# Layer 1's value rows in seven buffers, four of them borrowed from the rings of split up-projection weights

## The chip, the cores and the metric

The kernel runs on one core of one Trainium2 chip. The metric is the device time of the whole program in microseconds. The time before is the median of three runs, 2615.96 us (2612.59 to 2622.68).

## The reference

The program is a model of two layers over 256 tokens and 256 context tokens of width 1024. Each layer has a mixer (a convolution, a neighbourhood attention and a grouped attention over shared projections) and a PEER feed-forward, which is the part that matters here. For each token it picks, for each of 8 heads, 16 of 16384 experts by product keys, and then computes

```
act = gelu(einsum('cd,chkd->chk', xc, take(u, idx)))
out = einsum('chk,chkd->cd', g * act, take(v, idx))
```

so `u` and `v` are 16384 x 1024 tables of float32, `idx` are the picked experts and `g` the softmax of their scores. In the last layer only the 256 tokens go on, and the context does not.

## The kernel before

**How the work is tiled.** Most tokens are computed densely: the 16384 experts are cut into 128 blocks of 128, and each block is computed for all of these tokens, with a gate that is zero for experts that weren't picked. In layer 1 there are 192 dense token columns (`nd`): 128 of one tile and 64 of the other. The other 64 tokens take the rows of u and v that they picked by indirect DMA (names `gru` and `grv`), 64 steps each, and VectorE multiplies and sums them (L914, L921).

**A block of the sweep.** For block e, `act` multiplies the block's u (`raw_u`, 512 KB, plain float32) by the tokens in eight matmuls at L630, and ScalarE takes the gelu at L633 into `gact`. VectorE multiplies by the gates (L827; the gates come from DRAM as `gr`, eight blocks at a time, L825). ScalarE and VectorE split the product into two fp32r parts, `whi` (L831) and `wlo` (L832). The block's v (`raw_v`, 512 KB) is split in the same way into `hi_v` (L97) and `lo_v` (L99). For the first 128 tokens six fp32r matmuls (L119 to L121, into `acc`) multiply the parts; for the other 64 two plain ones at L842 use `raw_v` and `gact` themselves. In the texts U, R and A stand for the matmuls of L630, L842 and L119 to L121 of a block.

**Ahead of the sweep.** Layer 1 computes U of blocks 0 to 39 early, while VectorE still sorts and routes: eight stay in SBUF, 32 are spilled to DRAM (`gsp`, `spilled`) and come back as `gback` (L719). U of blocks 40 to 127 runs inside the sweep.

**Buffers.** All loads go through rings of `ring`, two or three buffers by tag:

```
raw = ring.tile(shape, F32, tag="raw" + kind, name="raw_" + nm, bufs=3)
hi = ring.tile(shape, F32R, tag="hi" + kind, name="hi_" + nm)
lo = ring.tile(shape, F32R, tag="lo" + kind, name="lo_" + nm)
```

Kind "v" has `rawv` (three buffers), `hiv` and `lov` (two each); kind "u" has `rawu`, `hiu` and `lou`. Each buffer holds 4 KB per partition. In layer 1 u isn't split, so nothing uses `hiu` and `lou` after the last split of the query weights (`piece(a["w_q"]...)`, L656). `rawv` is also used by the routing, for one-hot tiles (L792), up to the sweep's start.

**What sets the order.** Each engine, and SP's DMA queue, works through its instructions in one order, written when the program is built. The building tool places an instruction by its own estimate of when its operands and buffers will be free. A buffer's next load waits until the last reader of what it held is done, and all that stands behind it on SP waits with it. `hold` adds dependencies by hand: the gate product of block e waits for `wlo` of block e - 2, and a gather waits for the gate product of its block. The rings of `whi`, `wlo`, `hi_v` and `lo_v` have two buffers, so block e's need A of block e - 2 to be done.

Of the kernel before, what the change touches and what calls it, by code (L numbers as in the profile page):

```python
# [11 lines left out]
F32 = mybir.dt.float32  # L12
# [9 lines left out]
P = 128  # L22
T = 256
D = 1024
# [19 lines left out]
GA = {0: 4, 1: 8}  # L44
SPILL = {0: 42, 1: 32}
GLAG = 3
GB = 8
WOV = {0: (0, 1), 1: (1, 1)}
ZAT = (0, 2, 4, 6, 7, 9)
# [3 lines left out]
def hymba_kernel(ctx: ExitStack, tc: tile.TileContext, a, out):  # L53
    nc = tc.nc
# [4 lines left out]
    ring = ctx.enter_context(tc.tile_pool(name="ring", bufs=2))  # L59
# [26 lines left out]
    def hold(ins, after):  # L86

        if after is not None:
            tc.add_manual_dep(ins.ins, after.ins.name,
                              mybir.DependencyInfo(mybir.DependencyClass.Sync, mybir.DependencyReason.DATA),  # L90
                              reason="work that would crowd out more urgent work")


    def split(raw, shape, kind, nm, lo_eng=None, after=None):
        hi = ring.tile(shape, F32R, tag="hi" + kind, name="hi_" + nm)
        lo = ring.tile(shape, F32R, tag="lo" + kind, name="lo_" + nm)
        S.activation(hi, raw, AF.Copy)  # L97
        if lo_eng is None or lo_eng is V:
            V.tensor_tensor(lo, raw, hi.bitcast(F32), ALU.subtract)  # L99
        else:  # L100
            n = shape[1] // 4 if len(shape) == 3 and shape[1] == NC else 0
            for i in range(4):
                sl = (slice(None), slice(i * n, (i + 1) * n)) if n else (slice(None), i // 2, slice((i % 2) * 256, (i % 2 + 1) * 256))
                hold(lo_eng.tensor_tensor(lo[sl], raw[sl], hi[sl].bitcast(F32), ALU.subtract), after)  # L104
        return hi, lo

    def load(src, shape, kind, nm):
        raw = ring.tile(shape, F32, tag="raw" + kind, name="raw_" + nm, bufs=3)
        nc.sync.dma_start(raw, src)
        return raw  # L110
# [7 lines left out]
    def mm3(o, ahi, alo, bhi, blo, first, last):  # L118
        return [PE.matmul(o, lhsT=ahi, rhs=bhi, start=first, stop=False),  # L119
                PE.matmul(o, lhsT=ahi, rhs=blo, start=False, stop=False),  # L120
                PE.matmul(o, lhsT=alo, rhs=bhi, start=False, stop=last)]  # L121
# [17 lines left out]
    def squares(t, h):  # L139

        junk = cst.tile([P, 512], BF16, tag="sqj", name=f"sqj{t}{h}")
        S.activation(junk, resid[t][:, h * 512:(h + 1) * 512], AF.Square, accum_out=ssq[:, t, h:h + 1])
# [122 lines left out]
    def gate_rows(l, k, sets, tag="x2"):  # L265

        ns = mods[l][0].shape[-1] if len(sets) > 1 else 1
        ps = bank(tag, f"psrow{l}{k}")
        PE.transpose(ps[:NC * ns, :P], mod_of(l, k)[:, :, :ns].rearrange("p c s -> p (c s)"), ident)
        r = cst.tile([P, 256], F32, tag="sqj", name=f"gcol{l}{k}")  # L270
        S.activation(r[:NC * ns, :P], ps[:NC * ns, :P], AF.Copy)
        d = dram.tile([NC, ns, P], F32, name=f"growd{l}{k}")
        nc.sync.dma_start(d.rearrange("c s p -> (c s) p"), r[:NC * ns, :P])
        rows = {}
        for s in sets:
            rows[s] = cst.tile([P, D], F32, tag="grow", name=f"grow{l}{k}{s}", bufs=2)
            nc.sync.dma_start(rows[s].rearrange("p (c q) -> p c q", c=NC), d[:, s, :].partition_broadcast(P))
        return rows
# [311 lines left out]
    def peer(l):  # L590
# [120 lines left out]
        def act_of(e, sw, after):  # L711
# [5 lines left out]
            if i % 2 == 0:  # L717
                two[0] = sw.tile([P, 2, nd], F32, tag="gback", name=f"gback{l}_{e}", bufs=GB // 2)
                hold(nc.scalar.dma_start(two[0], spilled[:, i:i + 2, :]), after)  # L719
            return two[0][:, i % 2]  # L720

        sweep(l, dense, gath, act_of, h2n, eidx, gates, gd, nd, nb)

    def route(l, t, rt, rw, best, pos, tix, gate, gd, eidx, ntok):
# [84 lines left out]
    def sweep(l, dense, gath, act, h2n, eidx, gates, gd, nd, nb):  # L809
        sw = ctx_peer.enter_context(tc.tile_pool(name=f"sw{l}", bufs=2))  # L810
        pair = l == DEPTH - 1
# [9 lines left out]
        for e in range(NE):  # L821
            ga = act(e, sw, los[(e - GA[l]) // 2] if 0 <= e - GA[l] < GB else None)
            if e % EG == 0 and e >= NEAR[l]:
                gr = sw.tile([P, nb, EG, TB], F32, tag="gr", name=f"gr{l}_{e}")
                nc.scalar.dma_start(gr, gd[1][:, :, e:e + EG, :])  # L825
            g = gr[:, :, e % EG, :] if e >= NEAR[l] else gd[0][:, :, e, :]
            wi = V.tensor_tensor(ga[:, :nd].rearrange("p (b t) -> p b t", t=TB),  # L827
                            ga[:, :nd].rearrange("p (b t) -> p b t", t=TB), g, ALU.mult)
            whi = sw.tile([P, nw], F32R, tag="whi", name=f"whi{l}_{e}")
            wlo = sw.tile([P, nw], F32R, tag="wlo", name=f"wlo{l}_{e}")  # L830
            S.activation(whi, ga[:, :nw], AF.Copy)  # L831
            los.append(V.tensor_tensor(wlo, ga[:, :nw], whi.bitcast(F32), ALU.subtract))  # L832
            if e >= 2:
                hold(wi, los[e - 2])
            raw = load(a["v"][l, e], [P, D], "v", f"v{l}_{e}")
            v = split(raw, [P, D], "v", f"v{l}_{e}")

            def down_proj(j, h, e=e, whi=whi, wlo=wlo, v=v, ga=ga, raw=raw):
                ts, hs = slice(j * P, (j + 1) * P), slice(h * 512, (h + 1) * 512)
                if pair and j:  # L840

                    return [PE.matmul(acc[1][0][k * H:(k + 1) * H], lhsT=ga[:, P:P + H], rhs=raw[:, k * 512:(k + 1) * 512],  # L842
                                      start=e == 0, stop=e == NE - 1) for k in range(2)]
                return mm3(acc[j][h], whi[:, ts], wlo[:, ts], v[0][:, hs], v[1][:, hs], e == 0, e == NE - 1)

            if e < NE - 2:
                for j in range(len(dense)):
                    for h in range(len(acc[j])):
                        down_proj(j, h)
            else:  # L850
                last.append(down_proj)
            while steps and (e >= NE - 2 or ng - len(steps) < ng * (4 * e - 3 * min(e, ahead)) // (480 - 3 * ahead)):
                steps.pop(0)(wi)
            if e == NE - 12:
                rows = gate_rows(l, 5, [0, 1] if gath else [0], "mm")
            if e == NE - 2 and not pair:
                for g, t in enumerate(gath):
                    V.tensor_tensor(h2n[g], h2n[g], rows[t // 2], ALU.mult)
                    V.tensor_tensor(resid[t], resid[t], h2n[g], ALU.add)
                    for h in range(2):  # L860
                        squares(t, h)
# [22 lines left out]
        for j, t in [(1, 1), (0, 0)] if pair else enumerate(dense):  # L884
# [4 lines left out]
            if l == DEPTH - 1:  # L889
                y = sw.tile([P, D], F32, tag="grow", name=f"y{t}", bufs=GLAG + 1)  # L890
                y = [y[:, :512], y[:, 512:]]
# [7 lines left out]
    def gather_steps(l, gath, h2n, eidx, gates, sw, ns):  # L899
# [5 lines left out]
        def use(after):  # L905
            rows, f = waiting.pop(0)
            hold(f(rows), after)

        for g in range(len(gath)):
# [13 lines left out]
            def step(k, after, g=g, t=t, down=down, up=up):  # L923
                s = k % ns
                r = sw.tile([P, D], F32, tag="grow", name=f"gr{'uv'[k // ns]}{l}{t}{s}", bufs=GLAG + 1)
                d = G.indirect_dma_start(out=r, out_offset=None, in_=a["v_rows" if k >= ns else "u_rows"],  # L926
                                         in_offset=bass.IndirectOffsetOnAxis(ap=eidx[g][:, s:s + 1], axis=0))
                hold(d, after)
                waiting.append((r, lambda rows, s=s, f=up if k >= ns else down: f(s, rows)))
                if len(waiting) > GLAG:  # L930
                    use(after)
# [3 lines left out]
        if steps:  # L935
            steps.extend([use] * GLAG)
        return steps
# [89 lines left out]
```

## Time and profile before

| what | value |
|---|---|
| median of three runs | 2615.96 us |
| profiled execution, its own time | 2629.2 us |
| its span | 2627.1 us |
| PE busy | 95% of the span |
| DVE, ACT, POOL busy | 70%, 40%, 40% |
| HBM read, written | 628.63 MB, 49.44 MB |
| mean DMA rate | 259 GB/s |

Sums are made against the profiled execution, which is 13.2 us above the median. Engines: PE is TensorE's matmuls, PEld its weight loads, DVE VectorE, ACT ScalarE, POOL GpSimd, SP the queue that issues most loads. Layer 1's sweep runs from about 2005 us to 2615 us. An instruction's row gives its start, its length and, in brackets, how long its engine stood idle before it and what ended that. Neighbouring matmuls overlap, so the distance from start to start is what a matmul costs, not its length.

### The profile page before, as it was taken

To read this page: it belongs to the slowest core of one execution; us is meant where nothing else is said; L and a number is where in the kernel's file an instruction comes from. 1 tells how busy PE (TensorE), PEld (TensorE's weight loads), DVE (VectorE), ACT (ScalarE), POOL (GpSimd) and SP (SyncE) were. 2 spreads that over 40 slices of the span, in tenths; PEclk is the share of its full clock that TensorE was granted. 3 is DMA by queue.
4 is the path that set the end of the run, shared out by engine and by line. 5 is a ranking of instruction groups with operands and counts; after the bars stand their busy time and mean duration, and the time that the engine had idled before them with its cause. 6 is when DMAs were issued, how large, how long until landed. Compare 5 with 4: busy or idle time off the path is not lost. (4 is left out here: it accounts for less than half of the span.)

```text
span 2627.1 us, 38186 instructions
## 1 busy us (share of the span) xinstructions
PE 2491.1 (95%) x13837; PEld 2023.0 (77%) x13837; DVE 1831.6 (70%) x3506; ACT 1052.3 (40%) x1708; POOL 1050.9 (40%) x967
## 2 busy tenths in 40 slices
PE   7999999888899999999999998998998999999997
PEld 4755788877898888989989987855997756777775
DVE  1754589989546677787888885374994467666667
ACT  3345633367533333333333334445454333323323
POOL 3713434768642244454545441722600114223222
PEclk9999999999999999999999999998999999999999
DMA  7343364356878889999999992441579889999996
GB/s 270 104 169 122 127 245 145 119 211 263 311 257 276 293 295 328 326 343 339 347 331 342 338 336 85 161 164 49 159 241 344 278 286 326 377 356 361 350 366 234
DMA packets 263565, 681.42 MB, mean 259 GB/s; under 512 B 23840, under 2 KB 112976, under 8 KB 260304
## 3 DMA queue, kind: packets, MB, share of 16 engines
q1 hardware_dynamic: 121712, 423.48, 45.4%
q0 software_dynamic: 55296, 201.35, 20.8%
q10 hardware_dynamic: 86368, 54.15, 7.2%
q8 instruction: 109, 1.79, 0.3%
q14 instruction: 80, 0.66, 0.1%
HBM read 628.63 MB, written 49.44 MB: 258 GB/s over the span
## 5 line engine op out<-in xcount | busy, mean ns | idle before, releaser
L120 PE MATMUL acc<-lo_v,whi 128*128 128x512 f32 x1024 | 406.1, 397 | 2.9 <-DVE lo_v L99 2.8
L99 DVE TENSOR_TENSOR lo_v<-raw_v,hi_v 128x1024 fp32r<-128x1024 f32 x256 | 313.5, 1225 | 119.9 <-ACT hi_v L97 119.1
L630 PE MATMUL psu<-h2raw,raw_u 128*128 128x192 f32 x2048 | 364.9, 330 | 10.1 <-DMA raw_u<-in_u 6.3
L121 PE MATMUL acc<-hi_v,wlo 128*128 128x512 f32 x1024 | 374.4, 392 | 0.0
L97 ACT ACTIVATE hi_v<-raw_v 128x1024 fp32r<-128x1024 f32 x256 | 269.1, 1052 | 260.4 <-PE acc L121 234.5
L630 PEld LDWEIGHTS psu<-h2raw,raw_u 128*128 128x128 f32 x2048 | 339.8, 191 | 40.2 <-issue 20.7
L121 PE MATMUL psu<-ahi_m,lo_u 128*128 128x384 f32 x1024 | 351.7, 343 | 10.2 <-DVE lo_u L99 6.6
L119 PE MATMUL psu<-ahi_m,hi_u 128*128 128x384 f32 x1024 | 349.9, 342 | 7.0 <-ACT hi_u L97 2.9
L120 PE MATMUL psu<-alo_m,hi_u 128*128 128x384 f32 x1024 | 349.8, 342 | 0.0
L119 PE MATMUL acc<-hi_v,whi 128*128 128x512 f32 x1024 | 346.2, 404 | 2.9 <-ACT hi_v L97 2.7
L926 POOL DMA_INDIRECT gru<-in_u_rows,eidx x128 | 183.6, 1435 | 286.3 <-DVE gback L827 144.8
L119 PEld LDWEIGHTS acc<-hi_v,whi 128*128 128x128 f32 x1024 | 184.9, 188 | 104.1 <-ACT gact L633 55.2
L921 DVE SCALAR_TENSOR_TENSOR h2n<-grv,dots,h2n 128x1024 f32<-128x1024 f32 x190 | 243.0, 1279 | 26.0 <-DMA grv<-in_v,eidx 24.6
L914 DVE SCALAR_TENSOR_TENSOR gru<-gru,h2n 128x1024 f32<-128x1024 f32 x192 | 232.0, 1220 | 36.7 <-DMA gru<-in_u_rows,eidx 31.8
L104 POOL TENSOR_TENSOR lo_u<-raw_u,hi_u 128x256 fp32r<-128x256 f32 x184 | 213.1, 1190 | 95.2 <-ACT hi_u L97 84.0
L926 POOL DMA_INDIRECT grv<-in_v,eidx x128 | 171.3, 1338 | 188.3 <-DVE h2n L921 164.3
L926 POOL DMA_INDIRECT gru<-in_u_rows,egl x64 | 90.2, 1409 | 376.3 <-DMA spilled<-gsp 123.2
L120 PEld LDWEIGHTS acc<-lo_v,whi 128*128 128x128 f32 x1024 | 192.6, 188 | 55.8 <-issue 5.7
L121 PEld LDWEIGHTS acc<-hi_v,wlo 128*128 128x128 f32 x1024 | 192.3, 188 | 38.1 <-DVE wlo L832 0.3
L831 ACT ACTIVATE whi<-gact 128x128 fp32r<-128x128 f32 (+1 forms) x182 | 74.6, 410 | 337.2 <-PE acc L120 189.8
L121 PEld LDWEIGHTS psu<-ahi_m,lo_u 128*128 128x128 f32 x1024 | 195.7, 191 | 16.9 <-DVE lo_u L99 8.6
L119 PEld LDWEIGHTS psu<-ahi_m,hi_u 128*128 128x128 f32 x1024 | 195.8, 191 | 13.1 <-ACT gsp L633 3.5
(287 smaller groups left out, 4581.3 us busy)
## 6 DMA issues: line engine op xcount, KB each, us to landing
raw_u<-in_u SPq DMA_DIRECT2D x256, 512.0 KB, 5.6
raw_v<-in_v SPq DMA_DIRECT2D x256, 512.0 KB, 6.0
ada<-in_ada SPq DMA_DIRECT2D x96, 512.0 KB, 4.7
gd<-stage SPq DMA_DIRECT2D x24, 1024.0 KB, 5.5
gr<-gd ACTq DMA_DIRECT2D x16, 1536.0 KB, 25.2
raw_wq<-in_w_q SPq DMA_DIRECT2D x32, 512.0 KB, 3.6
raw_wout<-in_w_out SPq DMA_DIRECT2D x24, 512.0 KB, 3.5
gd<-stage SPq DMA_DIRECT2D x12, 960.0 KB, 5.8
```

The costliest lines, as they stand in the source:

```text
L97: S.activation(hi, raw, AF.Copy)
L99: V.tensor_tensor(lo, raw, hi.bitcast(F32), ALU.subtract)
L104: hold(lo_eng.tensor_tensor(lo[sl], raw[sl], hi[sl].bitcast(F32), ALU.subtract), after)
L119: return [PE.matmul(o, lhsT=ahi, rhs=bhi, start=first, stop=False), PE.matmul(o, lhsT=ahi, rhs=blo, start=False, stop=False), PE.matmul(o, ...
L120: PE.matmul(o, lhsT=ahi, rhs=blo, start=False, stop=False),
L121: PE.matmul(o, lhsT=alo, rhs=bhi, start=False, stop=last)]
L630: PE.matmul(ps[:, :nd], lhsT=u[:, c, :], rhs=h2raw[:, c, :nd], start=c == 0, stop=c == NC - 1)
L831: S.activation(whi, ga[:, :nw], AF.Copy)
L914: return V.scalar_tensor_tensor(r, r, 1.0, h2n[g], op0=ALU.mult, op1=ALU.mult, accum_out=dots[:, s:s + 1])
L921: return V.scalar_tensor_tensor(h2n[g], r, dots[:, s:s + 1], h2n[g], op0=ALU.mult, op1=ALU.add)
L926: d = G.indirect_dma_start(out=r, out_offset=None, in_=a["v_rows" if k >= ns else "u_rows"], in_offset=bass.IndirectOffsetOnAxis(ap=eidx[g ...
```

## The change

In layer 1 (`pair`) each v takes the next of seven buffers: two of `hiu`, two of `lou`, and the three of `rawv`. The tags repeat with period seven, so v of block e reuses the buffer of block e - 7. Nothing else is written differently; layer 0 loads as before. Line numbers are one higher in the changed kernel up to the new code in `sweep`, and seven higher behind it.

```diff
+VRING = (("hiu", 2), ("lou", 2), ("rawv", 3), ("hiu", 2), ("lou", 2), ("rawv", 3), ("rawv", 3))
...
-            raw = load(a["v"][l, e], [P, D], "v", f"v{l}_{e}")
+            if pair:
+
+                tag, bufs = VRING[e % len(VRING)]
+                raw = ring.tile([P, D], F32, tag=tag, name=f"raw_v{l}_{e}", bufs=bufs)
+                nc.sync.dma_start(raw, a["v"][l, e])
+            else:
+                raw = load(a["v"][l, e], [P, D], "v", f"v{l}_{e}")
             v = split(raw, [P, D], "v", f"v{l}_{e}")
```

The tool that builds the program writes another order for all engines but POOL from there on. On SP the first loads of u in layer 1 stand like this before (the number behind `raw_u_` is the block, the one behind it counts tiles):

```order
L109 DMA raw_wq_17662<-in_w_q 128x1024
L109 DMA raw_u_0_18440<-in_u 128x1024
L109 DMA raw_u_1_18453<-in_u 128x1024
L109 DMA raw_u_2_18466<-in_u 128x1024
L109 DMA raw_u_3_18479<-in_u 128x1024
L109 DMA raw_u_4_18492<-in_u 128x1024
```

and now:

```order
L110 DMA raw_wq_17662<-in_w_q 128x1024
L110 DMA raw_u_0_18440<-in_u 128x1024
L110 DMA raw_u_1_18453<-in_u 128x1024
L840 DMA raw_v_0_18974<-in_v 128x1024
L840 DMA raw_v_1_18993<-in_v 128x1024
L110 DMA raw_u_2_18466<-in_u 128x1024
L840 DMA raw_v_3_19031<-in_v 128x1024
L840 DMA raw_v_4_19052<-in_v 128x1024
L110 DMA raw_u_3_18479<-in_u 128x1024
L110 DMA raw_u_4_18492<-in_u 128x1024
```

Four loads of v, those that go into `hiu` and `lou`, moved from about sixty places further down to behind the last query weights.

PE in the middle of the sweep, around U of block 67, before:

```order
L630 MATMUL psu_66_20756<-h2raw_16632,raw_u_66_20757 128x192 x8
L842 MATMUL acc_18967<-raw_v_59_20518,gact_59_20511 64x512 x2
L119 MATMUL acc_18965<-hi_v_59_20520,whi_59_20514 128x512
L119 MATMUL acc_18966<-hi_v_59_20520,whi_59_20514 128x512
L120 MATMUL acc_18965<-lo_v_59_20521,whi_59_20514 128x512
L121 MATMUL acc_18965<-hi_v_59_20520,wlo_59_20515 128x512
L120 MATMUL acc_18966<-lo_v_59_20521,whi_59_20514 128x512
L121 MATMUL acc_18966<-hi_v_59_20520,wlo_59_20515 128x512
L630 MATMUL psu_67_20794<-h2raw_16632,raw_u_67_20795 128x192 x8
L842 MATMUL acc_18967<-raw_v_60_20556,gact_60_20549 64x512 x2
```

and now:

```order
L849 MATMUL acc_18967<-raw_v_66_20774,gact_66_20767 64x512 x2
L120 MATMUL acc_18965<-hi_v_66_20776,whi_66_20770 128x512
L121 MATMUL acc_18965<-lo_v_66_20777,whi_66_20770 128x512
L120 MATMUL acc_18966<-hi_v_66_20776,whi_66_20770 128x512
L121 MATMUL acc_18966<-lo_v_66_20777,whi_66_20770 128x512
L631 MATMUL psu_67_20794<-h2raw_16632,raw_u_67_20795 128x192 x6
L122 MATMUL acc_18965<-hi_v_66_20776,wlo_66_20771 128x512
L122 MATMUL acc_18966<-hi_v_66_20776,wlo_66_20771 128x512
L631 MATMUL psu_67_20794<-h2raw_16632,raw_u_67_20795 128x192 x2
L849 MATMUL acc_18967<-raw_v_67_20812,gact_67_20805 64x512 x2
```

Before, U of block 67 is followed by R and A of block 60; now R of block 67 itself is next. PE has 503 runs of U, R and A from block 29 on where it had 432, with the same matmuls in them.

DVE at the same place before (`lo_v` is the split of v, `gact_67<-gact_67,gr` the gate product of block 67, `gru` a sum over a gathered row):

```order
L832 TENSOR_TENSOR wlo_65_20736<-gact_65_20732,whi_65_20735 128x128
L827 TENSOR_TENSOR gact_67_20805<-gact_67_20805,gr_64_20697 128x192
L99 TENSOR_TENSOR lo_v_64_20707<-raw_v_64_20704,hi_v_64_20706 128x1024
L914 SCALAR_TENSOR_TENSOR gru_20678,dots_18968<-gru_20678,h2n_16630 128x1024
L832 TENSOR_TENSOR wlo_66_20771<-gact_66_20767,whi_66_20770 128x128
L827 TENSOR_TENSOR gact_68_20840<-gact_68_20840,gr_64_20697 128x192
```

and now:

```order
L833 TENSOR_TENSOR wlo_66_20771<-gact_66_20767,whi_66_20770 128x128
L100 TENSOR_TENSOR lo_v_67_20815<-raw_v_67_20812,hi_v_67_20814 128x1024
L921 SCALAR_TENSOR_TENSOR gru_20605,dots_18968<-gru_20605,h2n_16630 128x1024
L100 TENSOR_TENSOR lo_v_68_20850<-raw_v_68_20847,hi_v_68_20849 128x1024
L828 TENSOR_TENSOR gact_67_20805<-gact_67_20805,gr_64_20697 128x192
L921 SCALAR_TENSOR_TENSOR gru_20608,dots_18968<-gru_20608,h2n_16630 128x1024
L833 TENSOR_TENSOR wlo_67_20809<-gact_67_20805,whi_67_20808 128x128
```

The gate product of block 67 stood ahead of the splits of v of blocks 64 and 65; now it stands behind that of block 68, and only a sum is left between it and `wlo_67`.

## Rows read from the trace of the kernel before

**Rows 1.** The page's first part: busy us (share of the span) xinstructions by engine.

```profile
PE 2491.1 (95%) x13837; PEld 2023.0 (77%) x13837; DVE 1831.6 (70%) x3506; ACT 1052.3 (40%) x1708; POOL 1050.9 (40%) x967
```

**Rows 2.** Windows: us; busy us of PE, PEld, DVE, ACT, POOL; PEclk; DMA share; GB/s.

```profile
1875.00:1900.00 25.00, 23.98 (x183) 23.71 (x182) 25.00 (x170) 10.04 (x20) 9.67 (x14) 1.00 0.47 151
2000.00:2025.00 25.00, 19.55 (x85) 14.66 (x83) 5.59 (x13) 6.16 (x14) 1.05 (x1) 0.86 1.00 348
2125.00:2150.00 25.00, 22.55 (x94) 12.26 (x90) 15.42 (x25) 7.82 (x12) 5.40 (x3) 1.00 0.80 258
2150.00:2175.00 25.00, 21.73 (x86) 10.94 (x84) 18.88 (x32) 10.72 (x18) 6.42 (x4) 1.00 0.88 306
2400.00:2425.00 25.00, 25.00 (x128) 19.09 (x128) 17.37 (x22) 7.93 (x15) 8.26 (x7) 1.00 1.00 368
```

**Rows 3.** Timeline of PE in the sweep: start, us, operation [idle before <-releaser].

```profile
2003.64 4.52 PE L630 MATMUL psu<-h2raw,raw_u 128*128 128x192 f32 x16 [2.59 <-DMA raw_u<-in_u]
...
2021.77 0.79 PE L119 MATMUL acc<-hi_v,whi 128*128 128x512 f32 x1 [2.40 <-ACT hi_v L97]
...
2149.33 1.08 PE L842 MATMUL acc<-raw_v,gback 128*64 128x512 f32 x4 [2.42 <-DMA raw_v<-in_v]
...
2153.96 0.50 PE L120 MATMUL acc<-lo_v,whi 128*128 128x512 f32 x1 [0.53 <-DVE lo_v L99]
...
2157.22 1.08 PE L842 MATMUL acc<-raw_v,gback 128*64 128x512 f32 x4 [0.38 <-DVE wlo L832]
...
2167.64 1.94 PE L842 MATMUL acc<-raw_v,gback 128*64 128x512 f32 x8
...
2174.98 3.49 PE L842 MATMUL acc<-raw_v,gact 128*64 128x512 f32 x8 [2.36 <-DMA raw_v<-in_v]
...
2234.37 2.87 PE L630 MATMUL psu<-h2raw,raw_u 128*128 128x192 f32 x16 [1.69 <-DMA raw_u<-in_u]
...
2604.45 0.50 PE L120 MATMUL acc<-lo_v,whi 128*128 128x512 f32 x1 [1.25 <-DVE lo_v L99]
```

**Rows 4.** Waits of SP's own queue, 1850 to 2250 us.

```profile
SPq L109 <- DMA gr<-gd: 13.5, 1, 13.5
```

**Rows 5.** Timeline of PE over one block of the even stretch.

```profile
2401.06 2.76 PE L630 MATMUL psu<-h2raw,raw_u 128*128 128x192 f32 x16
...
2403.75 1.08 PE L842 MATMUL acc<-raw_v,gact 128*64 128x512 f32 x4
...
2404.76 0.73 PE L119 MATMUL acc<-hi_v,whi 128*128 128x512 f32 x2
...
2405.33 0.39 PE L120 MATMUL acc<-lo_v,whi 128*128 128x512 f32 x1
...
2406.25 2.76 PE L630 MATMUL psu<-h2raw,raw_u 128*128 128x192 f32 x16
```

**Rows 6.** Timeline of ACT there.

```profile
2403.85 0.33 ACT L633 ACTIVATE gact<-psu 128x192 f32<-128x192 f32 x1 [1.52 <-PE psu L630]
...
2406.28 0.31 ACT L831 ACTIVATE whi<-gact 128x128 fp32r<-128x128 f32 x1 [2.10 <-PE acc L120]
...
2406.50 1.04 ACT L97 ACTIVATE hi_v<-raw_v 128x1024 fp32r<-128x1024 f32 x1
```

**Rows 7.** Timeline of DVE there.

```profile
2406.62 0.29 DVE L832 TENSOR_TENSOR wlo<-gact,whi 128x128 fp32r<-128x128 f32 x1 [0.51 <-ACT whi L831]
...
2406.95 0.36 DVE L827 TENSOR_TENSOR gact<-gact,gr 128x192 f32<-128x192 f32 x1
...
2407.57 1.23 DVE L99 TENSOR_TENSOR lo_v<-raw_v,hi_v 128x1024 fp32r<-128x1024 f32 x1 [0.26 <-ACT hi_v L97]
...
2408.71 1.28 DVE L921 SCALAR_TENSOR_TENSOR h2n<-grv,dots,h2n 128x1024 f32<-128x1024 f32 x1
```

**Rows 8.** Timeline of PE: the wait before the sixth block of up-projections.

```profile
1907.87 2.52 PE L630 MATMUL psu<-h2raw,raw_u 128*128 128x192 f32 x10 [3.82 <-ACT gact L633]
```

**Rows 9.** Loads of u, 2200 to 2580 us, by tile: from issue to landing.

```profile
DMA to landing us min/median/max: 4.2/6.3/11.0
```

## The prediction

> **What bounds the kernel now.** I read the windows first, then PE's timeline at the idle spots that they showed, then what SP waited for, and last one block of the even stretch on PE, ACT and DVE. The page's first part says PE is the busiest engine, 2491.1 of 2627.1 us [rows 1]. The change touches layer 1's sweep alone, from about 2005 us on, and the loads ahead of it. In the sweep the windows show two kinds of stretch. From 2240 to 2600 us PE has no idle time and DMA is as full (25.00 of 25 us and a share of 1.00 at 368 GB/s, the last window of [rows 2]). Before that PE has gaps: 19.55 busy of 25 in 2000 to 2025, and 22.55 and 21.73 in 2125 to 2175, where DMA stands at 0.80 and 0.88 [rows 2]. PE's timeline names what ended each gap [rows 3]. Those from 2149 to 2175 are the ones a ring of three v buffers makes: spilled blocks need no u there, PE wants a v every 2.6 us, and it waits for raw_v itself (2.42, 2.36) or for what is made of it (0.53, 0.38).
>
> In the even stretch a block takes 5.19 us [rows 5]: eight up-projection matmuls of u (U, 2401.06 to 2403.75: 2.69), two raw matmuls (R, 1.01), six split ones (A, 1.49). What follows U of a block: gelu on ACT, starting 0.10 after U's slot, 0.33 long, and the gate product on DVE, 0.36 [rows 6, 7]. R can start after these, so about 0.9 us after U's end with a hop of 0.1. In the kernel before, U of block 67 stands seven blocks ahead of R of block 67, so nothing of this chain is seen.
>
> **The change part by part.** It adds no instruction and takes none away; 128 loads of v get four more buffers, and the scheduler writes another order.
>
> Early loads. v_0, v_1, v_3 and v_4 go in after the last query weights, ahead of u_2 and u_3. The four (2.1 MB) run where DMA is busy 0.47 of the time [rows 2]. u_2 and u_3 may come later by those loads, some 1.5 us each at 368 GB/s, but PE stands 3.82 us a little later for ACT, which waits for DVE [rows 8]; DVE is busy 25.00 of 25 there [rows 2]. I take 0; without that cover it would be up to 3.8. Between u_29 and u_33 as many v loads stand as before, so the gaps at 2003.64 and 2021.77 (2.59, 2.40 [rows 3]) stay. Behind raw_u the clock was low: U took 4.52 in place of 2.76 [rows 3, 5].
>
> Waits that go. By the orders of SP and PE, weighed with the durations of [rows 5], v's buffer is released 15 or more us of PE work ahead of v's use there, where it was 5 to 8. The four waits make 2.42 + 0.53 + 0.38 + 2.36 = 5.69 us, and after the last one eight records took 3.49 where they take 1.94: 1.55 more [rows 3]. Together -7.2. The wait of 1.69 at 2234 is not one of v's buffers: u was late, since SP stood 13.5 us for a load of gate rows (gr) [rows 4]. I leave it, at 0 (bounds -1.7 and 0). In the tail PE waits 1.25 for a lo_v that stands behind sums over gathered rows on DVE [rows 3]; in the new order those sums end before block 122's gate. -1.25. Gains: -8.5.
>
> The lead that goes. This is the cost. With v in plenty the scheduler lets the down-projections overtake: by PE's order the work between U of a block and R of the same block falls from 36 us (seven blocks' worth) to 2.6 us by block 59, and stays at 0 to 5.2 us up to the end. 2.6 us cover the chain. But at nine blocks it is 0.5 or less. At 62, 102 and 107 U stands directly ahead of R: 0.9 each, 2.7. At 74, 87 and 114 the split of the next v stands ahead of the gate on ACT and DVE, and it begins only when A of the block before frees its buffers: 1.04 + 1.23 + 0.36 [rows 6, 7] and 0.1 to 0.2 of hops make 2.75, less 1.35 of PE work (R and one U matmul): 1.4 each, 4.2. At 67 only 0.65 of PE work lies in it: 2.1. At 99 a gather sum of 1.28 [rows 7] stands there too, but with a whole U as cover: 1.4. At 90: 0.9 less two A: 0.45. Sum +10.9 (bounds 0, if DVE and ACT run ahead of their order's worst case, and 9 x 2.6 = 23, if each also meets a gather sum or late data).
>
> Switches. The first two A after R take 0.57 us where four further ones take 0.92, so a change of kind costs 0.11 [rows 5]. Such changes into R and A rise from 263 to 310 by PE's order: 47 x 0.1 = +4.7 (0 to 5.2).
>
> Sum: -8.5 + 10.9 + 4.7 = +7.1 us on the profiled execution's 2629.2, so 2636. That execution is 13.2 above the median of the runs, 2615.96; the same step on the median gives 2623.
>
> **The rivals.** *Faster: the order's tightness is free and the early loads pay.* The gates would be ready in time, since ACT and DVE stand idle 17 and 7.6 us of 25 [rows 2], and the fuller stock of v would also thin out DMA at 2000 to 2025 (share 1.00), so that 2.59, 2.40 and the 1.76 of low clock go: -8.5 - 6.8 - 1.7 + 4.7 = -12.3, 2604. Against it: the gate can't start before U's end, and the loads between those u's are unchanged in number.
>
> *Slower: u comes late.* In the new order two v stand ahead of most u on SP, and PE work from the release of a u buffer to its use falls from 13.0 to 9.9 at the least. The landing is 6.3 in the median and 11.0 at most [rows 9], and a gr load that lands late holds SP [rows 4]. It decides where the landing passes 10 us. From block 56 on there are nine gr loads; a case as at 2234 cost 1.69 with 14.0 us of cover, and would cost 5.3 with 10.4. If every second one does it: 4.5 x 5.3 = 24 more, 2647. For it: DMA at 1.00 [rows 2]; against it: the median, and PE that moves slower asks for less. The Trainium skill (DMA: Bandwidth & Descriptors, Issuing engines are not separate DMA queues) says that transfers of all issuing engines share the same 16 DMA engines, so v's longer queue would be paid by u and by the gathers. The trace agrees that they are full in this stretch.
>
> *Slower: each stop costs the clock.* After idle times of 2.59 and 2.36 the next matmuls ran at the lower level (4.52 against 2.76); after 2.42 and 1.69 they didn't (1.08, 2.87) [rows 3, 5]. If the nine stops each bring 1.76 more: 15.8, so 2639. It decides at stops of 2 us and more, and I count one such. The Trainium skill (TensorE: Matmul & The Clock Gate, HAM oscillation) says that gaps in PE's work bring the clock down to 1.2 GHz again and again, and that this is paid after each. By that rule the sum would be +23; by the rows, where two of the three waits for loads over 2 us did it and the short one did not, I keep +7.
>
> *It doesn't bring v earlier.* If the rings of split weights come free so late that v arrives as before, the 7.2 stays and the order's costs are paid: 2616 + 14.3 = 2630. Against it: SP's new order has v_0 right behind u_1, and the last query weights are used ahead of u_5, whose wait ends at 1907.87 [rows 8].
>
> **How the numbers follow.** Forecast 0.50 (its own range 2614 to 2631), faster rival 0.16, late u 0.14, clock 0.11, no earlier v 0.09. About 0.5%, 13 us, is what a measurement here can tell from no change: faster is under 2603, slower over 2629. Of the forecast 0.08 is slower and the rest same; of the faster rival 0.11 faster and 0.05 same; late u and clock are slower; no earlier v 0.06 slower, 0.03 same. So 0.11 faster, 0.50 same, 0.39 slower. The range 2606 to 2644 leaves out most of the faster rival's better half and the worse half of late u.
>
> **What would show it.** Right: PE idle in 2125 to 2175 gone, no wait for raw_v; from block 59 on some nine idle spots of 0.5 to 2 us before R, released by DVE's gate product; ACT's gelu right before the block's own whi; a block still 5.2 us between the spots. Wrong: no such spots (the first rival), waits of PE for raw_u in the late sweep (the second), PEclk under 1.00 there (the third), or waits for raw_v as before (the fourth).

## The result, and the profile after

The changed kernel takes 2638.4 us (2636.3 to 2640.5, six runs) where the kernel before takes 2616.8 (2610.2 to 2623.6, six runs): a ratio of 1.008, with a 95% interval of 1.0063 to 1.0098, so 21.6 us more. The forecast was 2623 on the median, so the size was 15 us short. The sign that it leaned to was right and the range of 2606 to 2644 holds the result, but the forecast's own 2614 to 2631 doesn't, and a time over 2629 is what the prediction called slower: it gave that 0.39, and 0.50 to no change.

The page's first part of the changed kernel answers to [rows 1]. Its profiled execution took 2637.4 us, its span is 2635.6. The same 13837 matmuls keep PE busy for 15 us more. The profiled execution of before lies 13 us above its median and this one 1 below, so the two spans don't give the difference as they stand. From the U that waited 2.59 us for raw_u (2003.64 in [rows 3], 1993.69 here) to the end of the span, the kernel before takes 623.5 us and the changed one 641.9: 18.4 more, all of it in the sweep.

```profile
PE 2506.1 (95%) x13837; PEld 2023.8 (77%) x13837; DVE 1827.1 (69%) x3506; ACT 1057.1 (40%) x1708; POOL 1047.0 (40%) x967
```

The windows of the changed kernel, with the columns of [rows 2]; the second and third, 2050 to 2100, were not shown of before.

```profile
2000.00:2025.00 25.00, 22.58 (x104) 14.71 (x102) 9.04 (x16) 7.32 (x13) 2.86 (x2) 1.00 1.03 357
2050.00:2075.00 25.00, 25.00 (x99) 14.42 (x98) 11.67 (x19) 7.49 (x13) 3.60 (x2) 1.00 0.83 285
2075.00:2100.00 25.00, 25.00 (x107) 15.61 (x106) 11.67 (x19) 7.22 (x13) 3.60 (x2) 1.00 0.66 221
2125.00:2150.00 25.00, 25.00 (x103) 14.37 (x104) 14.22 (x24) 8.95 (x14) 3.60 (x2) 1.00 0.85 293
2150.00:2175.00 25.00, 24.08 (x98) 13.23 (x94) 22.39 (x39) 10.69 (x19) 9.99 (x6) 1.00 0.92 326
2400.00:2425.00 25.00, 23.53 (x122) 18.17 (x124) 15.55 (x22) 7.11 (x14) 7.71 (x6) 1.00 0.97 349
```

And the kernel before in 2050 to 2100:

```profile
2050.00:2075.00 25.00, 25.00 (x127) 18.31 (x125) 13.14 (x22) 8.91 (x16) 3.60 (x2) 1.00 0.78 263
2075.00:2100.00 25.00, 25.00 (x119) 17.13 (x120) 12.86 (x22) 8.77 (x15) 3.60 (x2) 1.00 0.89 290
```

Two things are to be seen. From 2125 to 2150 the idle time is gone: 25.00 busy where [rows 2] have 22.55. And from 2050 to 2100 PE is busy without a gap in both kernels, at full clock, but it ends only 99 and 107 matmuls where it ended 127 and 119. The busy time says nothing there; the count behind it does. Matmuls are of several sizes, so the count is a hint, and the timeline below settles it.

All that PE waits for in the changed kernel, 1900 us to the end (us in total, times, longest):

```profile
PE acc L849 <- DVE gact L828: 11.0, 9, 2.0
PE psu L631 <- DMA raw_u<-in_u: 5.2, 3, 2.6
PE acc L120 <- ACT hi_v L98: 1.7, 1, 1.7
PE psu L631 <- ACT gact L634: 0.9, 1, 0.9
PE acc L121 <- DVE lo_v L100: 0.8, 1, 0.8
```

No wait for raw_v is left, and there are nine stops behind the gate product, as foretold. Where the matmuls went is in PE's timeline (start, us; a plain float32 matmul counts as two records, so R x4 is a pair of halves, R x2 one half):

```profile
2067.81 1.07 PE L849 MATMUL acc<-raw_v,gback 128*64 128x512 f32 x2
2068.81 0.73 PE L120 MATMUL acc<-hi_v,whi 128*128 128x512 f32 x2
2069.47 1.07 PE L849 MATMUL acc<-raw_v,gback 128*64 128x512 f32 x2
2070.48 0.50 PE L121 MATMUL acc<-lo_v,whi 128*128 128x512 f32 x1
...
2072.90 1.07 PE L849 MATMUL acc<-raw_v,gback 128*64 128x512 f32 x2
2073.90 0.73 PE L120 MATMUL acc<-hi_v,whi 128*128 128x512 f32 x2
```

From start to start a single half of R takes 1.00 (2067.81 to 2068.81, 2072.90 to 2073.90). A pair takes 1.01 (2403.75 to 2404.76 in [rows 5]). The two halves go to different 64 columns of the array, and as neighbours they run side by side; with two A between them each pays the full time. In the written order, runs of R with an odd number of halves rise from 8 to 44, most of them among blocks 8 to 56. Each costs half a pair, 0.505: 36 x 0.505 = 18.2.

### The profile page after: what moved, and what is told of

It is laid out like the page before. It is cut to its first block, busy times and chain, and to the rows that moved or that the text cites. A ratio compares the mean times of both kernels' runs of the same rounds, so it can differ in the third digit from the quotient of the medians.

```text
span 2635.6 us, 38151 instructions
## 1 busy us (share of the span) xinstructions
PE 2506.1 (95%) x13837; PEld 2023.8 (77%) x13837; DVE 1827.1 (69%) x3506; ACT 1057.1 (40%) x1708; POOL 1047.0 (40%) x967
## 5 line engine op out<-in xcount | busy, mean ns | idle before, releaser
L122 PE MATMUL acc<-hi_v,wlo 128*128 128x512 f32 x1024 | 368.1, 394 | 0.0
L120 PE MATMUL acc<-hi_v,whi 128*128 128x512 f32 x1024 | 358.1, 405 | 1.8 <-ACT hi_v L98 1.7
L928 DVE SCALAR_TENSOR_TENSOR h2n<-grv,dots,h2n 128x1024 f32<-128x1024 f32 x190 | 243.2, 1280 | 18.9 <-DMA grv<-in_v,eidx 18.2
L121 PEld LDWEIGHTS psu<-alo_m,hi_u 128*128 128x128 f32 x1024 | 196.4, 192 | 3.9
```

The costliest lines, as they stand in the source:

```text
L928: return V.scalar_tensor_tensor(h2n[g], r, dots[:, s:s + 1], h2n[g], op0=ALU.mult, op1=ALU.add)
```

## The experiments

Theory 1: the new order costs, by halves of R that are no longer neighbours (18) and by the lost lead (11), and the buffers give 8.5. Theory 2: the order costs, but by the lead and by changes between kinds of matmuls alone. Theory 3: the borrowed buffers themselves cost, through crowded DMA. The runs of e1 to e4 stood beside one set of runs of the kernel before (median 2618.3), those of e5 to e8 beside another (2617.5); ratios are to these.

**e1, seven buffers in the order of before.** A table holds TensorE's U, R and A, and each instruction follows the one ahead of it in the table; such an edge fixes the order on an engine.

```diff
+ORDER = """
+R0.0 R0.1 R1.0 R1.1 A0.00 A0.01 A0.10 A0.11 A0.02 A0.12 ...
+""".split()
...
+        if pair:
+            for x, y in zip(ORDER, ORDER[1:]):
+                follow(put[y], put[x])
```

> Seven buffers as in the changed kernel, but TensorE's U, R and A from the first R of layer 1 on are written in exactly the order of the kernel before. Theory 1 (the loss comes from the new order, above all from R's two halves that are no longer neighbours): only the gains are left, 2616.8 - 8.5 = 2608. Theory 2 (the loss comes from the new order, but from the lost lead and the changes of kind alone): also 2608. Theory 3 (the borrowed buffers themselves cost, by v loads that crowd the DMA engines and delay u): no gain, 2617 to 2638, with waits of PE for raw_u.

Measured 2610.0, ratio 0.9963 (0.9946 to 0.998). The buffers alone gain 8.3 us; theory 3 falls. PE's waits in e1, over the same stretch as above:

```profile
PE psu L721 <- DMA raw_u<-in_u: 4.5, 3, 2.3
PE psu L721 <- ACT gact L724: 3.9, 1, 3.9
PE acc L211 <- DVE lo_v L190: 2.7, 4, 0.7
```

The waits for raw_v are gone here too, and no stop stands behind the gate product.

**e2, halves apart in 40 blocks, and e3, more changes.** Both alter e1's table in blocks 70 to 109:

```diff
-R70.0 R70.1 A70.00 A70.10 A70.01 A70.02 A70.11 A70.12
+R70.0 A70.00 A70.10 A70.01 A70.02 A70.11 A70.12 R70.1
```

```diff
-R70.0 R70.1 A70.00 A70.10 A70.01 A70.02 A70.11 A70.12
+A70.00 A70.10 R70.0 R70.1 A70.01 A70.02 A70.11 A70.12
```

> As e1_order_of_before, and in 40 blocks of the even stretch (70 to 109) the second half of R stands behind the block's six A in place of ahead of them. The number of changes between plain and split matmuls stays 277. Theory 1 (a half without its neighbour costs as much as the pair, 0.505 more for each odd run; two odd runs of one block count 2 x 0.505): 40 x 2 x 0.505 less the two halves that the pair cost already, so 40 x 1.01 = 40.4 more if both halves take 1.00, and at least 40 x 0.505 = 20.2 if one of the two hides under a neighbour: 2628 to 2648. Theory 2 (only changes of kind and the lead count): 2608, as e1_order_of_before.

> As e1_order_of_before, and in the same 40 blocks two of the six A stand ahead of R, whose halves stay neighbours. That makes 357 changes between plain and split matmuls in place of 277. Theories 1 and 2: 80 x 0.106 = 8.5 more than e1_order_of_before, so 2617. If any cut into R and A cost as much as a pair pulled apart, it would be as slow as e2_halves_apart.

Measured: e2 2654.3 (1.014, 1.0116 to 1.0165), 44.4 more than e1; e3 2611.7 (0.9968, 0.9953 to 0.9982), 1.7 more, within the intervals. One block of e2 on PE (L941 is R):

```profile
2409.78 1.07 PE L941 MATMUL acc<-raw_v,gact 128*64 128x512 f32 x2
2410.79 0.72 PE L210 MATMUL acc<-hi_v,whi 128*128 128x512 f32 x2
...
2412.37 1.07 PE L941 MATMUL acc<-raw_v,gact 128*64 128x512 f32 x2
2413.37 2.87 PE L721 MATMUL psu<-h2raw,raw_u 128*128 128x192 f32 x16
2416.17 1.07 PE L941 MATMUL acc<-raw_v,gact 128*64 128x512 f32 x2
```

and one of e3:

```profile
2413.54 0.76 PE L210 MATMUL acc<-hi_v,whi 128*128 128x512 f32 x2
2414.24 1.08 PE L941 MATMUL acc<-raw_v,gact 128*64 128x512 f32 x4
2415.24 0.50 PE L211 MATMUL acc<-lo_v,whi 128*128 128x512 f32 x1
...
2418.74 0.76 PE L210 MATMUL acc<-hi_v,whi 128*128 128x512 f32 x2
```

With both halves alone the block takes 6.39 (2409.78 to 2416.17), 1.20 more than the 5.19 of [rows 5]: 1.00 for the second half, and 0.2 that A and U take longer behind the two halves (1.58 and 2.80, where [rows 5] have 1.49 and 2.69). With a pair in another place it takes 5.20 (2413.54 to 2418.74). Cutting A in two is free here; pulling the pair apart is not. These two runs tell theory 1 from theory 2. e3 also corrects the price of a change of kind, 0.106 in its expectation: 80 more of them cost 8.5 by it, and 1.7 was measured.

**e4, the order of the change with the halves rejoined.** The table of the changed kernel's order, R's second half moved behind its first:

```diff
-A7.12 R8.1 R9.0 R9.1 R10.0 R10.1
+A7.12 R9.0 R9.1 R10.0 R10.1
```

(R8.1 now stands behind R8.0, further up.)

> Seven buffers and the order of the changed kernel, with one thing altered: R's second half stands right behind its first in every block, so the odd runs of R go from 44 to 0 and the changes of kind from 347 to 337. Theory 1: 44 x 0.505 = 22.2 and 10 x 0.106 = 1.1 less than the changed kernel's 2638.4, so 2615; the nine stops behind the gate product stay, about 11 us. Theory 2: 2637.

Measured 2618.5 (1.0005, 0.9991 to 1.0019): 20 us less than the changed kernel, where theory 1 said 23 and theory 2 one. Its windows in 2050 to 2100 have the matmuls back:

```profile
2050.00:2075.00 25.00, 25.00 (x124) 17.68 (x119) 13.76 (x25) 8.65 (x16) 3.61 (x2) 1.00 0.90 301
2075.00:2100.00 25.00, 25.00 (x121) 17.10 (x119) 14.75 (x25) 9.13 (x17) 5.41 (x3) 1.00 0.80 271
```

The stops behind the gate product stay. e1 has none of them, and they are more than the 8.5 us that separate e4 from e1 by the medians:

```profile
PE acc L941 <- DVE gact L920: 12.0, 10, 2.0
```

**e5, the lead kept.** U is written two blocks ahead, and R and A may not overtake it:

```diff
+            while len(gas) <= min(e + lead, NE - 1):
+                n = len(gas)
+                gas.append(act(n, sw, los[(n - GA[l]) // 2] if 0 <= n - GA[l] < GB else None))
+            ga = gas[e]
...
+                if pair and ahead <= e + lead < NE:
+                    follow(ins[0], ulast[e + lead])
```

> Seven buffers; R and A of a block from 38 on may stand no earlier than behind U of the block two further on, so 5 us and more of TensorE's work lie between U of a block and its R everywhere. The halves are left to the order: 34 odd runs of R in place of 44. Theory 1 (halves 0.5 for each odd run, stops at the gate product 11, and 0.1 for each change between U, R and A as the traces price them): 2638.4 - 11.0 - 10 x 0.5 - 6.4 = 2616, with no stop of PE behind the gate product. If the halves were the whole loss: 2638.4 - 5 = 2633. If the lead were the whole loss: 2610.

Measured 2623.0 (1.0018, 1.0 to 1.0036). No stop behind the gate product is left in its waits. It is 15.4 below the changed kernel: 11.0 of stops and 10 odd runs of 0.5 make 16.0. The 6.4 that the expectation added for changes of kind are not there, as in e3. The halves that stay apart show in its window of 2075 to 2100, x99 again:

```profile
2075.00:2100.00 25.00, 25.00 (x99) 14.34 (x98) 9.97 (x17) 6.89 (x12) 2.23 (x2) 1.00 0.66 226
```

**e6, three buffers in the order of the change.** The kernel before, with the changed kernel's table in e1's code.

> Three buffers as in the kernel before, and TensorE's U, R and A in exactly the order of the changed kernel. Theory 1 (the order costs, the buffers give): the changed kernel's 2638.4 and the 8.3 that the buffers give back on top: 2647, with waits for raw_v and for what is made of it in the middle. Theory 3 (the buffers cost): 2617.

Measured 2670.6 (1.0198, 1.0174 to 1.0222). The order does cost without the buffers, but by 53 us, not 30. The waits for v are most of the miss:

```profile
PE acc L934 <- DMA raw_v<-in_v: 18.5, 11, 4.5
PE acc L934 <- DVE gact L919: 11.6, 11, 3.5
```

18.5 in eleven waits where before had 4.8 in two: 13.7 of the 23 us. Behind the longest of them the granted clock was 0.62 (2190 to 2195 us), which is part of the rest. An order written for plenty of v asks for v sooner than three buffers can bring it. So buffers and order don't add up: seven buffers are worth 8.3 us in the old order and 32 in the new one.

**e7, three buffers, halves joined.** The kernel before, and R's second half follows its first and is written with priority. The edit also carries the code of e5 for a lead of two blocks; U stays seven blocks ahead of R all the same.

```diff
+                    a0 = half(0)
...
+                    with tc.high_priority():
+                        a1 = half(1)
+                    follow(a1, a0)
```

> Three buffers as in the kernel before, R's two halves always neighbours (8 odd runs to 0), U's lead as it was (seven blocks). Theory 1: 2617 - 8 x 0.5 - 0.6 for fewer changes = 2612.5; the waits for raw_v stay. If halves count for nothing: 2617.

Measured 2616.5 (0.9999, 0.9983 to 1.0014): a miss, or too small to see. PE's waits from 1900 us on are 22.7 us in e7 and 20.2 in the kernel before. Those for hi_v are ten, where before has three of 2.7 in all:

```profile
PE acc L124 <- ACT hi_v L102: 5.6, 10, 2.7
```

Eight of the ten, of 0.25 to 0.36 us, stand between 2280 and 2570, where the kernel before has no idle time. Behind such a wait A is cut around a whole U (2329.70 to 2332.73), where it stands together in [rows 5]. The order thus differs in more than the halves, and e7 doesn't price the eight of them by itself.

**e8, all three: seven buffers, halves joined, a lead of two blocks.** The edits of e5 and e7 on the changed kernel.

> Seven buffers, R's halves always neighbours, and the lead of two blocks as in e5_lead_kept: what the theory says is best. A of a block stands ahead of its R in the even stretch. Theory 1: from the kernel before 2617 - 8.3 (waits for v) - 4 (odd runs) - 7.4 (changes of kind, 0.23 into R from U and 0.11 into A from R against 0.14 into A from U and 0.10 into R from A) = 2597, with no stop behind the gate product. If the price of the changes is not that: 2605. If a lead of two blocks is too short for the data of A: waits for wlo or lo_v, 2610 and more.

Measured 2601.9 (0.9943, 0.9924 to 0.9962): the fastest of all, 15.6 below the kernel before and 36.5 below the changed one. Its ratio overlaps e1's, so that it beats e1 isn't shown. PE's waits and its first part of the page:

```profile
PE 2479.2 (95%) x13837; PEld 2018.4 (78%) x13837; DVE 1829.6 (70%) x3506; ACT 1052.8 (40%) x1708; POOL 1039.9 (40%) x967
```

```profile
PE psu L636 <- DMA raw_u<-in_u: 5.9, 4, 2.7
PE psu L636 <- ACT gact L639: 4.7, 2, 3.8
PE acc L125 <- ACT hi_v L103: 1.1, 1, 1.1
PE acc L126 <- DVE lo_v L105: 0.8, 1, 0.8
```

The same matmuls take 27 us less of PE than in the changed kernel. The 7.4 that the expectation took off for changes of kind is not to be seen: a block of the even stretch still takes 5.19 (from R to R, 2398.47 to 2403.66), and without that term it said 2605.

## Why the prediction was right or wrong

*Early loads, 0.* Not tested by itself. The wait of 3.82 that was to cover them came again at that length (at 1897.60), and so did the wait of 2.59 for raw_u and the 4.52 behind it, at a granted clock of 0.62 (1993.70 to 1998.20):

```profile
1993.69 4.52 PE L631 MATMUL psu<-h2raw,raw_u 128*128 128x192 f32 x16 [2.59 <-DMA raw_u<-in_u]
```

*Waits that go, -8.5.* Right in size: e1, which has nothing else, gains 8.3 (5 to 14 by its interval). By the waits of e1 it is in part luck. The two for raw_v and the slow matmuls behind the second are gone, as foretold. But the 0.53 for lo_v stayed (at 2142.71), 0.73 came beside it (2163.47), and the tail's 1.25 fell only to 0.66; and two waits that were counted to stay, 2.40 for hi_v and 1.69 for u, are not in e1's profile.

*The lead that goes, +10.9.* Right, in number, place and size: nine stops, 11.0 us. Single ones are off by up to 0.6 (that of block 74 took 2.04 where 1.4 was foretold), and this cancels in the sum. That of block 67, priced at 2.1, is the second of them:

```profile
2292.68 1.08 PE L849 MATMUL acc<-raw_v,gact 128*64 128x512 f32 x4 [2.02 <-DVE gact L828]
```

DVE there, with lo_v of the next block ahead of the gate product, as the order said:

```profile
2291.14 1.23 DVE L100 TENSOR_TENSOR lo_v<-raw_v,hi_v 128x1024 fp32r<-128x1024 f32 x1 [2.18 <-ACT hi_v L98]
2292.28 0.35 DVE L828 TENSOR_TENSOR gact<-gact,gr 128x192 f32<-128x192 f32 x1
```

e5 takes the stops away and is faster by as much as they and its ten odd runs amount to.

*Switches, +4.7.* This is the step that failed. It counted the pieces that the order is cut into, at 0.1 each, and in effect took R for two matmuls of 0.505 that add up wherever they stand. The row that it rests on, R at 1.01 in [rows 5], is a pair. It doesn't say what one half costs, and the prediction didn't ask. A lone half was to be found in the trace of before, which has eight odd runs: there one takes 1.01 as well:

```profile
2118.41 1.07 PE L842 MATMUL acc<-raw_v,gback 128*64 128x512 f32 x2
2119.42 0.50 PE L120 MATMUL acc<-lo_v,whi 128*128 128x512 f32 x1
```

In the place of 4.7 stand 18 (36 odd runs x 0.505; 20 by e4 for all 44). More pieces of A are worth next to nothing (e3). More pieces of R weren't tested apart from the halves: their runs rise from 124 to 136 in the tables of e1 and e6, which at the 0.2 of e2 would be 2.4 us, too little to tell.

The Trainium skill (TensorEngine Tiling (Array Packing), Key Properties) says that different tiles of the array can execute in parallel. The trace agrees, with 1.01 for a pair and 1.00 for one half.

With the measured sizes the sum closes: -8.3 + 11.0 + 18.2 = +20.9, against 21.6 by the medians. It takes the buffers in the old order first (e1) and the new order on top of them; by e6 the two don't simply add.

That the range held 2638.4 is luck. Its upper part stood there for the rivals "late u" and "clock", and neither came but for one stop; the clock rival even named 2639, by a cost that it counted nine times. The two terms that were right make -8.3 + 11.0 = +2.7 of the 21.6.

*The rivals.* Late u didn't come: PE waits 5.2 us for raw_u in three waits, all by 1994 us, and none later in the sweep. The clock paid at one stop of nine, that of 1.78. R behind it took 1.67 and U 3.55, some 1.5 us more together than at full clock, at a granted clock of 0.58 (2546.70 to 2549.00):

```profile
2546.76 1.74 PE L849 MATMUL acc<-raw_v,gact 128*64 128x512 f32 x4 [1.78 <-DVE gact L828]
2548.43 3.85 PE L631 MATMUL psu<-h2raw,raw_u 128*128 128x192 f32 x16
2551.98 0.53 PE L120 MATMUL acc<-hi_v,whi 128*128 128x512 f32 x1
```

The prediction counted one too, but expected it at the stops of 2 us and more, which kept the clock (1.08 at 2292.68 and at 2332.39). Its tally of before was of waits for loads alone; behind the 2.40 for hi_v the granted clock was low too, 0.50 (2021.70 to 2026.00). The faster rival failed by the stops and the halves; "no earlier v" by the waits for raw_v that are gone.

What stays open: what lowers the clock behind one stop and not behind another, where the 3 us between 2605 and e8's 2601.9 come from (its interval is wider than that), and why the tool parts the halves in this order and seldom in the old one.

## What to carry to other kernels

More buffers let the tool that builds the program write another order, so such a change is two changes: its buffers are judged by a run in the old order, and its order by a run of its own. Count what a fully busy engine ends in a window, not only how long it is busy, and ask of every duration in the sum which neighbours it was measured with. Matmuls that share the array are to be tied together in the code, and a consumer of a chain over two other engines is to be held a block or two behind its producer.

## What the hardware showed beyond that

A half of 64 columns between other matmuls takes 1.00 us and a pair of neighbours 1.01. A block that goes into R twice pays some 0.2 beside that (e2), while further changes between plain float32 and fp32r matmuls, with R's pair left whole, show no price that these runs can measure (e3: 80 of them, 1.7 us).

And the length of a stop didn't decide the clock. Of the two levels, 1.2 and 2.4 GHz, the matmuls behind the stops of 1.78 and 2.59 ran mostly at the lower (0.58 and 0.62 of full speed in the stretches given above), while the granted clock stayed at 1.00 behind 3.47 in e6 (2325 to 2330). The same stop, 2.02 ahead of R of block 67, kept it at 1.00 in the changed kernel and was followed by 0.66 in e4, from U on. First the changed kernel, by the columns of [rows 2], then e4, then the stop in e6:

```profile
2292.68:2297.68 5.00, 5.00 (x26) 3.96 (x27) 3.59 (x7) 0.45 (x2) 3.02 (x3) 1.00 0.75 268
```

```profile
2284.00:2289.00 5.00, 5.00 (x17) 3.82 (x18) 3.59 (x7) 0.29 (x1) 3.03 (x3) 0.66 0.77 262
2284.00 1.08 PE L941 MATMUL acc<-raw_v,gact 128*64 128x512 f32 x4 [2.02 <-DVE gact L920]
2285.01 1.42 PE L721 MATMUL psu<-h2raw,raw_u 128*128 128x192 f32 x4
```

```profile
2325.02 1.08 PE L934 MATMUL acc<-raw_v,gact 128*64 128x512 f32 x4 [3.47 <-DVE gact L919]
```
